# The last 128 maxima of a row-norm kernel: four small transposes and one 512-byte line for one transpose and four short rows

## Chip, cores, metric

One core of one Trainium2 chip. The metric is the time of one execution as measured on the device, in microseconds (us), from a few runs of each kernel. The trace's own span, from the program's first instruction to its last, is a little shorter. The runs list spans to 0.1 us, so a time minus span from a run without a trace is good to 0.05 us. The experiments ran on two chips (the fifth to the eighth on another than the rest), each beside the kernel before in the same rounds.

Some terms. A semaphore is a counter by which engines and copies tell one another that work is done; raising it is an increment. The issue of a copy is the instruction that starts it; the data move afterwards, in packets. The closing barrier is the meeting of all engines at the program's end. The TensorE clock was granted in full in every run.

## Reference

```python
def reference(x: np.ndarray) -> np.ndarray:      # x: 8192 x 8192 float32
    return np.linalg.norm(x, ord=np.inf, axis=1) # the largest |x| of every row
```

256 MiB (268.44 MB) are read, 32 KiB are written.

## The kernel before

Rows go to partitions, 128 at a time. 25 large loads (128 partitions x 16384 values) are followed by ever smaller ones, so that little is left to do when the last byte lands. Each load is reduced by one VectorE instruction. SyncE issues all DMA copies. The cuts of code below are shortened; `...` marks what is left out.

```python
class Pieces:
    ...
    def reduce(self, dst, src):
        i = len(self.reductions)
        ins = self.nc.vector.tensor_reduce(out=dst, in_=src, axis=X, op=max, apply_absolute_value=True)
        ins.wait_op(self.sems[i % SEMS], 16 * (i // SEMS + 1), "sem-ge")
        ...
```

The maxima of all rows but the last 128 are turned by TensorE and stored while the last pieces are still being reduced (`store_early`). The last 128 lie one per partition, in the first column of `last`, and are turned at the very end:

```python
    last_t = single.tile([P, 32], f32)
    make_identity(nc, ident)
    ...
    store_early()

    turn = nc.vector.transpose(out=last_t, in_=last)     # 4 blocks of 32x32
    pieces.after_loads(turn)
    tc.declare_fence(turn.ins, group="loads")
    nc.sync.dma_start(
        out=out_tail[n_tail - 1].rearrange("(b k) -> b k", k=32),
        in_=last_t.rearrange("(b c) k -> c b k", c=32)[0],   # partitions 0, 32, 64, 96
    )
```

A VectorE transpose turns every block of 32x32 by itself. So the 128 maxima end up as four rows of 32 values (128 B), in partitions 0, 32, 64 and 96, and go out as a 4x32 copy.

## Time and profile before

| | before |
|---|---|
| time, median of 4 runs | 630.83 us (630.74 to 630.91) |
| profiled run: time, span | 630.54 us, 628.346 us |
| VectorE busy | 88% |
| HBM read | 268.44 MB, 427 GB/s |
| instructions in VectorE's compiled program | 65 |

The lines that carry the reading stand in the prediction below: the loads fill the DMA engines to the end, VectorE keeps step, and after the last reduction a string of 2.76 us runs alone. From the view of the closing barrier's line in the kernel before (engine, operation, count: shortest/median/longest ns, start of the first and of the last in us; the q after the engine's name means its sequencer):

```profile
L224 DVEq EVENT_SEMAPHORE  x2: 21/21/21, 627.8 to 628.3; - x2
L224 PEldq EVENT_SEMAPHORE  x2: 51/51/51, 627.8 to 628.3; - x2
```

Every engine passes that barrier together.

### The profile page before, as it was taken

What the parts mean: (1) busy time and instruction counts of PE and PEld (TensorE: products, weight loads), DVE (VectorE), ACT (ScalarE), POOL (GpSimd) and SP (SyncE); (2) the same over time, 40 slices, a digit from 0 to 9 for tenths busy, and PEclk for the clock granted to TensorE, in tenths of its full rate; (3) what the DMA queues carried; (4) which work ended last, traced back from release to release, by engine and by line L of the source; (5) the groups of instructions that cost most, each with busy time, mean ns of one, the idle gap of its engine ahead of it and who ended that gap; (6) DMA issues with size and microseconds to landing.
All of it is one profiled execution on the core that took longest, in us unless ns stands there. A gap on an engine that the chain in (4) does not pass through costs nothing.

```text
span 628.3 us, 182 instructions
## 1 busy us (share of the span) xinstructions
PE 1.0 (0%) x3; PEld 0.3 (0%) x3; DVE 551.9 (88%) x54; ACT 2.0 (0%) x4; POOL 3.2 (1%) x15
## 2 busy tenths in 40 slices
PE   0000000000000000000000000000000000000000
PEld 0000000000000000000000000000000000000000
DVE  0588988889988889888898888998888999999998
ACT  0000000000000000000000000000000000000000
POOL 0000000000000000000000000000000000000000
DMA  9999999999999999999999999999999999999996
GB/s 401 401 467 401 467 401 467 401 467 401 467 401 467 401 467 401 467 401 467 401 467 401 467 401 467 401 467 401 467 401 434 434 434 434 434 414 428 424 424 281
DMA packets 7696, 268.47 MB, mean 427 GB/s; under 512 B 874, under 2 KB 912, under 8 KB 1936
## 3 DMA queue, kind: packets, MB, share of 16 engines
q1 hardware_dynamic: 7696, 268.47, 99.2%
HBM read 268.44 MB, written 0.03 MB: 427 GB/s over the span
## 4 chain that ended last, share of the span: by engine, by line
DMA 55%; DVE 44%; issue 0%; DVEq 0%
DMA ring<-in_x_dram 55%; DVE res_big L88 25%; DVE res_tail L88 10%; DVE parts L88 8%; DVE ring L88 1%; DVE last_t L194 0%; DVEq L88 0%
## 5 line engine op out<-in xcount | busy, mean ns | idle before, releaser
L88 DVE TENSOR_REDUCE res_big<-ring 128x2 f32<-128x16384 f32 x25 | 430.5, 17220 | 73.7 <-DMA ring<-in_x_dram 73.7
L88 DVE TENSOR_REDUCE res_tail<-ring 128x1 f32<-128x8192 f32 x7 | 60.2, 8675 | 0.0
L88 DVE TENSOR_REDUCE parts<-ring 128x1 f32<-128x4096 f32 (+5 forms) x15 | 52.2, 3555 | 0.0
L88 DVE TENSOR_REDUCE ring<-ring 128x1 f32<-128x1408 f32 (+4 forms) x6 | 9.1, 1566 | 0.1
L188 POOL TENSOR_SCALAR res_tail<-parts 128x1 f32<-128x1 f32 x6 | 1.7, 283 | 602.4 <-DVE parts L88 602.4
L151 ACT COPY line<-ps 25x128 f32<-25x128 f32 x2 | 0.5, 264 | 502.8 <-PE ps L150 502.8
L150 PE MATMUL ps<-ident,res_big 128*25 128x128 f32 x2 | 0.6, 402 | 504.4 <-DVE res_big L88 504.4
L151 ACT ACT_TABLE_LOAD x1 | 1.3, 1283 | 0.7 <-PEq L213 0.7
L188 POOL TENSOR_SCALAR parts<-parts 128x1 f32<-128x1 f32 x3 | 0.8, 282 | 10.7 <-DVE parts L88 10.7
L159 ACT COPY line_tail<-ps_tail 13x128 f32<-13x128 f32 x1 | 0.3, 255 | 112.1 <-PE ps_tail L157 112.1
L157 PE MATMUL ps_tail<-ident,res_tail 128*13 128x128 f32 x1 | 0.4, 391 | 112.0 <-POOL res_tail L188 112.0
L150 PEld LDWEIGHTS ps<-ident,res_big 128*25 128x25 f32 x2 | 0.2, 124 | 504.4 <-issue 504.4
masks.py:199 POOL TENSOR_SCALAR_AFFINE_SELECT ident<-ident 128x128 f32<-128x128 f32 x1 | 0.3, 294 | 0.1
L194 DVE STREAM_TRANSPOSE last_t<-ring 128x32 f32<-128x32 f32 x1 | 0.2, 211 | 0.0
masks.py:197 POOL MEMSET ident<- 128x128 f32 x1 | 0.2, 205 | 0.3 <-POOLq L213 0.3
L157 PEld LDWEIGHTS ps_tail<-ident,res_tail 128*13 128x13 f32 x1 | 0.1, 97 | 112.5 <-POOL res_tail L188 112.5
L213 POOL MEMSET const-uint8-127<- 128x1 uint8 x1 | 0.1, 103 | 0.0
L213 POOL MEMSET const-bfloat16-1.0<- 128x1 bf16 x1 | 0.1, 102 | 0.0
L213 POOL MEMSET const-float32-0.0<- 128x1 f32 x1 | 0.1, 99 | 0.2 <-issue 0.2
L213 POOL MEMSET const-float32-1.0<- 128x1 f32 x1 | 0.1, 99 | 0.0
## 6 DMA issues: line engine op xcount, KB each, us to landing
ring<-in_x_dram SPq DMA_DIRECT2D x7, 4096.0 KB, 40.5
ring<-in_x_dram SPq DMA_DIRECT2D x8, 2048.0 KB, 39.0
ring<-in_x_dram SPq DMA_DIRECT2D x2, 1216.0 KB, 27.7
ring<-in_x_dram SPq DMA_DIRECT2D x2, 864.0 KB, 23.3
ring<-in_x_dram SPq DMA_DIRECT2D x1, 1664.0 KB, 26.6
ring<-in_x_dram SPq DMA_DIRECT2D x2, 704.0 KB, 15.1
ring<-in_x_dram SPq DMA_DIRECT2D x1, 1248.0 KB, 20.9
ring<-in_x_dram SPq DMA_DIRECT2D x1, 1120.0 KB, 19.3
```

The source lines that it names most:

```text
L88: ins = self.nc.vector.tensor_reduce(out=dst, in_=src, axis=mybir.AxisListType.X, op=mybir.AluOpType.max, apply_absolute_value=True,)
L150: nc.tensor.transpose(ps, res_big[:, :, r], ident)
L151: nc.scalar.copy(out=line[:, :, r], in_=ps)
L157: nc.tensor.transpose(ps, res_tail, ident)
L159: nc.scalar.copy(out=line_tail, in_=ps)
L188: nc.gpsimd.tensor_scalar(out=dst, in0=best, scalar1=parts[i], scalar2=None, op0=mybir.AluOpType.max)
L194: turn = nc.vector.transpose(out=last_t, in_=last)
L213: nc = _bacc.Bacc("TRN2", target_bir_lowering=False, num_devices=1)
```

## The change

The intent: let the store be one full line of 512 B instead of four short ones. Four transposes of one 32x32 block each write side by side into 32 partitions, so that all 128 maxima come to lie in partition 0.

```diff
-    last_t = single.tile([P, 32], f32)
+    last_t = single.tile([32, P], f32)
...
-    turn = nc.vector.transpose(out=last_t, in_=last)
-    pieces.after_loads(turn)
+    for b in range(P // 32):
+        turn = nc.vector.transpose(
+            out=last_t[:, b * 32 : b * 32 + 32], in_=last[b * 32 : b * 32 + 32, :]
+        )
+        pieces.after_loads(turn)
     tc.declare_fence(turn.ins, group="loads")
     nc.sync.dma_start(
-        out=out_tail[n_tail - 1].rearrange("(b k) -> b k", k=32),
-        in_=last_t.rearrange("(b c) k -> c b k", c=32)[0],
+        out=out_tail[n_tail - 1].rearrange("(b k) -> b k", b=1),
+        in_=last_t[0:1, :],
     )
```

## The prediction

> **What bounds the kernel now.** I read the page's shares and its chain first, to see what kind of kernel this is; then the timeline and the chain of the last microseconds, because all that the diff touches runs there; then the DMA queue's own waits, for what follows the store.
>
> The page says that 268 MB are read and that the DMA engines are 90% busy or more in every slice but the last:
>
> ```profile
> DMA  9999999999999999999999999999999999999996
> HBM read 268.44 MB, written 0.03 MB: 427 GB/s over the span
> ```
>
> So the loads set the time almost to the end, and VectorE (88% busy) keeps step with them. A change behind the last load can touch only what lies behind it. That is the end of the timeline (start us, us, engine, line, operation, tiles):
>
> ```profile
> 617.70 0.33 SPq L160 DMA_DIRECT2D out_dram<-line_tail  x1
> 625.62 0.21 DVE L194 STREAM_TRANSPOSE last_t<-ring 128x32 f32<-128x32 f32 x1
> 625.86 0.60 SPq L197 DMA_DIRECT2D out_dram<-last_t  x1
> ```
>
> and of the chain that ended last:
>
> ```profile
> 616.49 7.71 DVE ring L88 x5
> 624.20 0.03 issue
> ...
> 624.30 1.30 DVE ring L88
> 625.60 0.02 issue
> 625.62 0.21 DVE last_t L194
> ```
>
> The reader should see two things. One: from 616 us on VectorE has no gap worth a name, so the last reduction ends at 625.6 because VectorE works, not because it waits (the semaphore of the last load is full at 624.04, before the last reduction starts at 624.30). Two: after it comes one serial string to the end of the span at 628.3: transpose, issue of the store, the store's journey, the closing barrier. Nothing lies beside it. The waits of the DMA queue show the journey and who waits for it:
>
> ```profile
> SPq L197 <- DVE last_t L194: 7.8, 1, 7.8
> SPq L160 <- ACT line_tail L159: 5.5, 1, 5.5
> SPq L224 <- DMA out_dram<-last_t: 0.9, 1, 0.9
> ```
>
> From the trace's single packets and semaphore events I take the string in finer steps (us from the span's start): transpose 625.622 to 625.833; issue 625.862 to 626.461; four packets of 128 B, which start at 627.090, 627.097, 627.118 and 627.150 and take 11 ns each, each followed by its 4-byte semaphore write, the last done at 627.167; their four increments seen at 627.417 to 627.481; the closing barrier goes on at 627.497 and ends at 628.346. Every part of the change is therefore paid or gained in full, and the whole string from 625.62 on is 2.7 us, 0.4% of the time. That is the frame: the time cannot move by 2% (12.6 us) unless something breaks.
>
> **What the Trainium skill says.** Four places.
> "VectorE: DVE Perf Modes", section "Two Vector instructions with no wait between them": an instruction is held until all earlier ones have finished if its input starts in another group of 32 partitions than the last input did (or its output than the last output). The four new transposes read partitions 0, 32, 64 and 96 on, so the second, third and fourth would be held. The trace of before has only the unheld kind: its last 1408-wide reduction but one runs 1.609 us and the next starts 1.527 us after its start, an overlap of 0.08 us.
> "DMA: Bandwidth & Descriptors", section "Why a DMA increments its semaphore by 16 and not by 1": the store's outer count sets how many engines carry it, and the issuing sequencer adds the rest. The trace agrees: 4 rows give four data packets, four increments by engines and one by the sequencer (626.87). One row should give one packet on one engine.
> The same page, "Specifications": writes under 512 B cost a read-modify-write. The trace has no equal write of 512 B with idle engines to compare with, so I can't tell what that costs here.
> "Perfetto Trace Analysis", section "DMA Instruction — HWDGE (DVE, Sync)": the profiled issue ends when the sequencer is done, and the data movement lies outside it. The trace agrees: the issue ends at 626.46, the first packet starts 0.63 us later.
>
> **The change, part by part.**
> The order of instructions against the kernel before shows nothing moved: the one 128x32 transpose becomes four 32x32 at the same place on VectorE, the store from 4x32 becomes 1x128, and all waits stay as they are; only the fourth transpose raises a semaphore, and the store waits for it.
>
> Transposes. A 32x32 transpose streams 32 elements per partition, as the 128x32 one did; with fewer partitions it should be no shorter, so 211 ns each. Held, one after another with the 20 to 35 ns that the trace shows between the last reduction and the transpose: three more at 211 + 25 = 0.24 us, sum +0.71 us. Not held, they would be one per (60 + 32 x 1.04 =) 93 ns, by the constants that the kernel's own author fitted for the reductions, which 1.527 us for 1408 columns confirms: sum +0.28 us. I lean to held, but the gap may be nearly nothing: +0.65 us.
>
> Issue of the store. The store of before is the dearest issue in the program: 599 ns. All others with an earlier wait take 327 to 376 ns, and the nearest in form, line_tail from 13 rows of consecutive partitions, takes 332. What sets last_t apart is that its four rows lie 32 partitions apart. The compiled programs differ there too: of the 56 DMA copies before, last_t's alone lacks a mark (ant_dge_precooked) that the others carry; after, it has it as well. So I expect about 330 ns: -0.27 us. This is the part that the change's words do not mention.
>
> The journey. One packet in place of four: the fourth one started 60 ns after the first, and that stagger goes; the one packet is 512 B, where 512-byte packets of loads took 27 to 29 ns against 11: net about -0.04 us. The confirmation (0.31 us from the end of a semaphore packet to its increment) I leave as it is. Whether a write of 512 B is confirmed sooner I can't size; I take 0 to -0.1 us, and put nothing in the sum.
>
> Sum: +0.65 - 0.27 - 0.04 = +0.34 us. On 630.75 that is 631.09; I shade it for the unsized confirmation and say 631.05.
>
> **The rivals.**
> The transposes overlap as the reductions do: +0.28 - 0.27 - 0.04 = -0.03 us, a tie at 630.7. For it: the reductions of before overlap by 0.08 us. Against: they never change partition group, these do.
> The store gains more than expected, because a full 512-byte line saves the read-modify-write that the change is after: with -0.3 us more the sum is +0.04 us, a tie again. For it: the string's longest pause, 0.9 us from issue to release. Against: of that 0.9 us, 0.63 us pass before the first packet starts, and the 0.31 us of confirmation are the most that could shrink.
> The issue does not become cheaper (599 ns may come from something else, such as the engines having gone idle since 624 us): +0.61 us, 631.35. For it: it is the only issue whose engines stood idle for over a microsecond. Against: the first loads of the program, also on idle engines, took 402 to 432.
> The loads themselves run otherwise in the new kernel: nothing in the order of instructions changes for them, so I give it no weight beyond the scatter of runs (630.74 to 630.91, and 630.54 in the profiled one).
>
> **Range and chances.** All rivals lie between -0.1 and +0.7 us; the scatter of one kernel adds some 0.2 on each side, and another chip or day may add a little more: 630.5 to 631.7. A move of over 2% would need 12.6 us, over four times the whole string behind the last reduction; I leave 1% on each side for what I have not seen.
>
> **What would show it.** Right: a group of four transposes at about 211 ns, the last one ending some 0.9 us after the last reduction (0.25 us before); an issue of about 330 ns for last_t; one packet of 512 B; a span of about 628.6 us. Wrong: transposes that start under 0.15 us apart (overlap, so no loss), an issue that still takes 0.6 us (then the row spacing is not what made it dear), or a confirmation clearly under 0.3 us (then the short writes did cost something). If the span differs by more than a microsecond, the loads have changed, and my frame is wrong.

## The result

| | before | after |
|---|---|---|
| time, median | 630.83 us (4 runs, 630.74 to 630.91) | 630.39 us (4 runs, 630.30 to 630.52) |
| profiled run: time | 630.54 us | 630.30 us |
| profiled run: span | 628.346 us | 628.620 us |
| time minus span | 2.194 us | 1.680 us |
| VectorE's program | 65 instructions | 68 instructions |

The ratio of the times is 0.9993 (95% interval 0.9976 to 1.0011): the same within 2%. Ratios here are the mean time of one kernel's fast runs over the mean of the other's in the same rounds, so not quite the ratio of the medians quoted. The predicted 631.05 was 0.66 us too high, and 630.39 lies 0.11 us below the predicted range.

The odd thing stands in the table: **the span became longer by 0.27 us, and the time shorter.** The profiled span came out where it was predicted (628.6), in part by luck: 0.10 of its +0.27 us is a later last reduction. What fell is the part of the time that lies outside the span.

From the timeline of the kernel after:

```profile
625.73 0.84 DVE L196 STREAM_TRANSPOSE last_t<-ring 32x32 f32<-32x32 f32 x4
626.59 0.23 SPq L201 DMA_DIRECT2D out_dram<-last_t  x1
```

The transposes take 0.84 us instead of 0.21, as foreseen, but the issue takes 0.23 us where 0.33 was expected and 0.60 was before. From the DMA queue's own waits in the kernel after:

```profile
SPq L201 <- DVE last_t L196: 8.4, 1, 8.4
SPq L228 <- DMA out_dram<-last_t: 0.8, 1, 0.8
```

The wait for the store to land is 0.8 us, 0.1 less than before. And from the closing barrier's line:

```profile
L228 DVEq EVENT_SEMAPHORE  x2: 21/21/21, 628.0 to 628.6; - x2
L228 PEldq EVENT_SEMAPHORE  x2: 51/51/51, 628.0 to 628.5; - x2
```

Here VectorE's last instruction starts at 628.6, the others' at 628.5; before, both were at 628.3. In the single events VectorE starts 0.13 us behind the other engines. That is a first hint at VectorE's instruction stream.

With the trace's single packets and semaphore events the string behind the last reduction can be added up, in us:

| piece | before | after | change |
|---|---|---|---|
| transposes, first start to last end | 0.211 | 0.840 | +0.629 |
| start of the store's issue to its first packet | 1.228 | 0.700 | -0.528 |
| first packet to end of the last | 0.077 | 0.036 | -0.041 |
| last packet to its increment | 0.314 | 0.328 | +0.014 |
| three short hand-overs | 0.079 | 0.078 | -0.001 |
| closing barrier, to the end of the span | 0.849 | 0.946 | +0.097 |
| time minus span | 2.194 | 1.680 | -0.514 |
| sum, from the end of the last reduction to the end of the time | 4.952 | 4.608 | -0.344 |

(In the profiled run of after the last reduction itself ended 0.104 us later, so the profiled times differ by only 0.24. The end of that reduction moves by 0.1 to 0.6 us from run to run of one kernel, with the loads. The sum of the last line is free of that, and I use it below as "the tail".) The time minus span lies behind the span: the last event on the semaphore by which the engines meet comes 2.314 us after the span's end before, and 1.807 us after it in the kernel after, a difference of 0.507 us.

So the change itself is nearly a tie inside the program (+0.17 us), and half a microsecond goes after its end. Why?

### The profile page after: what moved, and what is told of

Read it like the earlier page. It is cut to its first block, busy times and chain, and to the rows that moved or that the text cites. A ratio compares the mean times of both kernels' runs of the same rounds, so it can differ in the third digit from the quotient of the medians.

```text
span 628.6 us, 185 instructions
## 1 busy us (share of the span) xinstructions
PE 1.0 (0%) x3; PEld 0.3 (0%) x3; DVE 552.5 (88%) x57; ACT 2.0 (0%) x4; POOL 3.2 (1%) x15
## 4 chain that ended last, share of the span: by engine, by line
DMA 55%; DVE 44%; issue 0%; DVEq 0%
DMA ring<-in_x_dram 55%; DVE res_big L88 25%; DVE res_tail L88 10%; DVE parts L88 8%; DVE ring L88 1%; DVE last_t L196 0%; DVEq L228 0%; DVEq L88 0%
```

## The experiments

Theory A: VectorE's program is three instructions longer, and this moves the place at which its next block of instructions has to be fetched, from behind the closing barrier, where it delays everyone, to before it, where it is hidden. Theory B: it is the store, of which less is left to settle when the program ends. Every run lists time and span, so time minus span can be read in each.

### Three idle instructions, and nothing else

```diff
     make_identity(nc, ident)
+    pad = single.tile([P, 3], f32)
+    for i in range(3):
+        nc.vector.memset(pad[:, i : i + 1], 0.0)
```

> The kernel before with three memsets of one column on VectorE at the program's start, where VectorE waits for the first load: nothing of the last microseconds is touched, but VectorE's program is 68 instructions long as in the kernel after, not 65. The time measured on the device is longer than the span in the trace by 2.2 us before and by 1.7 us after. Theory (the gain is the place at which the longer VectorE program ends, nothing of the transposes or the store): span as before, 628.3 to 628.6, but time minus span falls to 1.7, so the time falls by about 0.5, to 630.3. Rival (the gain comes from the store, of which less is left to settle when the program ends): span and time as before, 630.8, time minus span 2.2.

Measured: 630.24 us (630.10 to 630.34) against 631.04 of the kernel before in the same rounds, ratio 0.9989 (0.9974 to 1.0004). Time minus span was 1.67 to 1.74 us in all four runs, against 2.14 to 2.26 in the seven runs of before. The timeline at the end is that of the kernel before, only shifted by 0.04 us:

```profile
625.66 0.21 DVE L197 STREAM_TRANSPOSE last_t<-ring 128x32 f32<-128x32 f32 x1
625.90 0.60 SPq L200 DMA_DIRECT2D out_dram<-last_t  x1
```

Old transpose, old store, short end. B falls, and of A the length of the program is borne out (that a fetch lies behind it is tested further below): three memsets that compute nothing, at the start of the program, make the whole gain outside the span. The interval of the ratio includes 1, so the times alone would not show it. The tail, free of the loads, is 4.541 us here against 4.952 before: the length is worth 0.41 us net, because 0.11 of the 0.52 outside comes back as a longer closing barrier.

### Half of the change at a time

The four transposes with the store of before:

```diff
-    turn = nc.vector.transpose(out=last_t, in_=last)
+    for b in range(P // 32):
+        turn = nc.vector.transpose(out=last_t[b * 32 : b * 32 + 32, :], in_=last[b * 32 : b * 32 + 32, :])
...
     nc.sync.dma_start(out=out_tail[n_tail - 1].rearrange("(b k) -> b k", k=32),
         in_=last_t.rearrange("(b c) k -> c b k", c=32)[0])
```

> The four transposes of the change alone, with the store of before (4 rows of 128 B, 32 partitions apart). Both theories: transposes 0.84 us instead of 0.21, issue of the store 0.6 us, so the span is 0.6 longer than before, about 629.0. Theory of VectorE's program length (68): time minus span 1.7, time about 630.7. Rival (the store): time minus span 2.2, time about 631.4.

Measured: 630.93 us against 631.04, time minus span 1.63 to 1.73.

```profile
626.14 0.85 DVE L196 STREAM_TRANSPOSE last_t<-ring 32x32 f32<-32x32 f32 x4
627.02 0.60 SPq L201 DMA_DIRECT2D out_dram<-last_t  x1
```

The span was 629.1 to 629.6, as expected or a little longer.

The store of the change with one transpose (three quarters of the line are zeros):

```diff
-    last_t = single.tile([P, 32], f32)
+    last_t = single.tile([P, P], f32)
     make_identity(nc, ident)
+    nc.gpsimd.memset(last_t[:, 32:P], 0.0)
...
-    turn = nc.vector.transpose(out=last_t, in_=last)
+    turn = nc.vector.transpose(out=last_t[:, 0:32], in_=last)
...
+    nc.sync.dma_start(out=out_tail[n_tail - 1].rearrange("(b k) -> b k", b=1), in_=last_t[0:1, :])
```

> The store of the change alone: one 128x32 transpose, then one line of 512 B, of which only the first 32 values are right (wrong on purpose; the rest is a memset to 0 early on GpSimd, which makes the programs of GpSimd and SyncE one instruction longer, VectorE's stays at 65). Issue 0.23 us, first packet 0.7 us after the issue starts instead of 1.23, so the span is about 0.55 shorter than before, 627.9. Theory of VectorE's program length: time minus span 2.2, time about 630.2. Rival (the store): time minus span 1.7, time about 629.7.

Measured: 630.22 us against 631.04, time minus span 2.14 to 2.23, span 627.9 to 628.5.

```profile
625.79 0.21 DVE L195 STREAM_TRANSPOSE last_t<-ring 128x32 f32<-128x32 f32 x1
626.09 0.23 SPq L198 DMA_DIRECT2D out_dram<-last_t  x1
```

With this the square is closed: old or new store, 65 or 68 instructions, and time minus span follows the number of instructions alone. In the tail, the transposes alone cost 0.64 us against the padded kernel before (5.183 to 4.541), and the new store alone gains 0.50 us against the kernel before (4.456 to 4.952), although its issue started 0.092 us after the transpose here and 0.029 before.

### What made the old store dear

The store of before, from partitions 0 to 3 instead of 0, 32, 64, 96:

```diff
-        in_=last_t.rearrange("(b c) k -> c b k", c=32)[0],
+        in_=last_t[0:4, :],
```

> The kernel before with its store of four 128 B rows taken from partitions 0 to 3 instead of 0, 32, 64, 96 (wrong on purpose). The compiled copy now carries the mark that all other copies carry. If the dear issue came from the missing mark or the row spacing: issue about 0.33 us instead of 0.60, first packet about 0.25 to 0.5 us earlier, span and time 0.3 to 0.5 lower. If it came from the number or the size of the rows: issue 0.6, nothing changes. Time minus span 2.2 by the theory of program length (VectorE 65).

Measured: 630.42 us against 631.04, time minus span 2.21 to 2.23.

```profile
626.25 0.25 SPq L197 DMA_DIRECT2D out_dram<-last_t  x1
```

Still four rows of 128 B, but the issue fell to 0.25 us and the first packet came 0.72 us after its start, not 1.23. Neither the number of rows nor their size was dear.

The same rows with the copy's mark switched off:

```diff
+    nc.dge_precook = False
     nc.sync.dma_start(
```

> The previous kernel (store from partitions 0 to 3, wrong on purpose) with the mark switched off for that one copy, so same rows, same sizes, adjacent, but unmarked. If the missing mark is what makes the issue dear: issue back at 0.60 us (marked: 0.25), first packet 1.22 us after the issue starts (marked: 0.72), span 0.5 above the marked one's. If the row spacing is: all as in the marked one. Time minus span 2.2 either way (VectorE 65 instructions).

Measured: 630.76 us against 630.75, first packet 1.32 us after the start of the issue, each 0.1 us more than expected (issue 0.70).

```profile
626.05 0.70 SPq L198 DMA_DIRECT2D out_dram<-last_t  x1
```

Same bytes, same rows, and all of the cost is back. (The mark is a flag that the build puts on a copy. Built once more, the two kernels' programs differ in one byte, in this copy's instruction.) So it is the missing mark in the compiled copy that is dear, and the spacing of 32 partitions because the build gave no mark to a copy with such rows; rows so spaced with the mark, in one copy, were not run. Its worth is 0.60 us up to the first packet for these rows, of which only 0.45 us (0.70 to 0.25) show in the issue's own duration.

### The length of VectorE's program

Two idle memsets, as above with 2 for 3:

> The kernel before with two idle memsets at VectorE's start, so 67 instructions. In the three kernels with 68, VectorE's very last instruction comes 0.13 us late, which none with 65 shows: if a block of instructions has to be fetched there, the fetch falls at the last instruction with 68, and with 67 or less behind the program's end, where it delays the closing work. Theory (a fetch at a fixed place of the stream): with 67 still time minus span 2.2, time as before, and no late last instruction. Rival (the delay falls gradually with length): time minus span about 1.85.

Measured: 630.66 us against 630.75, time minus span 1.94 to 2.00. Neither expectation was met to the number. The theory said 2.2 and the rival 1.85, so the passage from 2.2 to 1.7 is not one sharp step between 67 and 68: at 67 part of the delay is already gone. VectorE's last instruction was not late, as the theory said.

Twelve:

> The kernel before with twelve idle memsets at VectorE's start, so 77 instructions. Theory (a fetch at a fixed place): the fetch now falls among the last reductions, while earlier instructions run, so it is hidden wholly: time minus span 1.7 and no late last instruction, so the span is about 0.1 shorter than with three memsets, time 0.1 lower. Rival (only certain lengths are short, or the effect grows with length): time minus span 2.2 again, or well under 1.7. If the fetch delays a reduction, a gap of up to 0.5 us shows between the last reductions.

Measured: 631.52 us against 630.75, by the medians slower by 0.77 (ratio 1.0008, 0.9993 to 1.0023), though time minus span was 1.79 to 1.83 and VectorE's last instruction was not late. The part outside the span was 0.1 us above the theory's 1.7, but the 0.1 us by which the late last instruction lengthens the closing barrier with 68 is gone: barrier and outside together take 2.62 us here and 2.63 in the kernel after, against 3.04 before. The part inside the span did not meet the theory. A fetch of instructions now stands in the view of the DMA queues, where the kernel before has only q1 (queue, kind: packets, MB, share):

```profile
q1 hardware_dynamic: 7696, 268.47, 99.0%
q14 instruction: 1, 0.01, 0.0%
```

and among the waits after 560 us, where VectorE of the kernel before waits for no load:

```profile
DVE parts L88 <- DMA ring<-in_x_dram: 0.6, 2, 0.3
```

The fetch, one packet of 8192 B, starts at 564.2 us, amid the loads. The next load to land did so 3.09 us before its reduction started; in the kernel before it was 3.86. The loads behind it have little to spare (0.43 us, then 0.08 for the tightest), and so two reductions waited for their load. The two gaps, with the overlap lost, are 0.72 us. So what left the program's end was not free here: at the fetch the landing of the loads falls back by another 0.76 us against the kernel before (from 0.71 to 1.47), and stays there. That the fetch does this is argued from the moment, and how one packet of 0.33 us costs so much is not shown. The profiled span is longer by 1.48 us in all; the other 0.70 us arose by the fifth load, before 101 us. That is the scatter of the loads: the second run of the padded kernel below (3 memsets) fell back by 0.6 us between its third load and its sixth, with no fetch in its span.

Three memsets on GpSimd:

```diff
-        nc.vector.memset(pad[:, i : i + 1], 0.0)
+        nc.gpsimd.memset(pad[:, i : i + 1], 0.0)
```

> The three idle memsets on GpSimd instead of VectorE: GpSimd's program 39 instructions for 36, VectorE's 65. Theory (VectorE's length alone counts, because VectorE's fetch is the one that is not hidden): time minus span 2.2, time as before. Rival (any engine's longer program, or the memsets' work, does it): time minus span 1.7.

Measured: 630.73 us against 630.75, time minus span 2.15 to 2.22. It is VectorE's length that counts, not any memsets, and not GpSimd's. (In the version with two queues below, SyncE's and ScalarE's programs are longer too, and time minus span is that of 68.)

### Are the transposes held?

```diff
-            out=last_t[:, b * 32 : b * 32 + 32], in_=last[b * 32 : b * 32 + 32, :]
+            out=last_t[:, b * 32 : b * 32 + 32], in_=last[0:32, :]
```

> The kernel after with all four transposes reading partitions 0 to 31 (wrong on purpose: one quarter four times). In the kernel after they start 0.212 us apart. If they are held because each reads another group of 32 partitions than the one before: now not held, starts about 0.09 us apart, the four together 0.48 us instead of 0.84, span and time 0.36 lower. If a transpose never overlaps the one before: 0.212 apart, nothing changes. Time minus span 1.7 (VectorE 68).

Measured: 629.98 us against 630.74, ratio 0.9986 (0.9972 to 0.9999). The result was wrong on purpose, one quarter of the maxima four times, though close enough in value to pass the comparison with the reference.

```profile
625.77 0.48 DVE L196 STREAM_TRANSPOSE last_t<-ring 32x32 f32<-32x32 f32 x4
```

The starts are 0.135, 0.094 and 0.093 us apart instead of 0.212, 0.214 and 0.212. The change of the partition group is what keeps the four apart, and it costs 0.36 us of the change's 0.63. (The four also read the same bytes here; the two were not separated.)

### The two kernels at equal length, and a version meant to beat both

> The kernel after once more, on the same chip as the next two, to compare it with the kernel before at equal length of VectorE's program. Theory: time minus span 1.7, time 0.4 to 0.5 below before.

Measured: 630.24 us (630.21 to 630.58) against 630.74, ratio 0.9992 (0.9979 to 1.0005), time minus span 1.64 to 1.74.

> The kernel before with three idle memsets on VectorE, beside the kernel after on one chip: both have 68 instructions on VectorE. By the trace the change by itself costs 0.63 us in transposes, gains 0.53 up to the first packet and 0.04 in packets, so this one should be 0 to 0.15 us faster than the kernel after. If the change has a gain of its own beyond the program's length, the kernel after is faster than this one.

Measured: 630.40 us (630.36 to 630.95), time minus span 1.65 to 1.70. By the medians the kernel after is 0.16 us faster, against the expectation; behind the last reduction the traces have it slower. The last reduction ended at 626.2 us in the profiled run of this one and at 625.6 in the other, and the same program had run with its last reduction ending at 625.6 the first time; that is the scatter of the loads. Behind the last reduction the tail is 4.538 us here (4.541 the first time) and 4.616 in the kernel after (4.608 the first time): the change by itself costs 0.07 us. Single times can't resolve that; the traces agree with each other to 0.01.

```diff
     turn = nc.vector.transpose(out=last_t, in_=last)
...
+    row = out_tail[n_tail - 1].rearrange("(b k) -> b k", k=32)
+    for b in range(P // 32):
+        eng = nc.sync if b % 2 == 0 else nc.scalar
+        eng.dma_start(out=row[b : b + 1], in_=last_t[b * 32 : b * 32 + 1, :])
```

(and the three memsets on VectorE)

> A version meant to beat both: one 128x32 transpose as before, the four rows stored by four marked copies of 128 B, two issued by SyncE and two by ScalarE, and three idle memsets on VectorE. Each issue 0.23 us, so the last first-packet comes about 0.95 us after the transpose instead of 1.26: about 0.3 us below the padded kernel before, 629.95. Rival: the two queues' issues do not run beside each other, then 4 times 0.23 and no gain over the padded kernel before. Time minus span 1.7 in both, if the longer programs of SyncE and ScalarE do not matter.

Measured: 630.34 us (630.17 to 630.60), time minus span 1.70 to 1.77. The expected gain of 0.3 us did not come, as the rival said: the tail is 4.641 us, 0.10 more than the padded kernel's.

```profile
626.23 0.52 SPq L203 DMA_DIRECT2D out_dram<-last_t  x2
626.24 0.81 ACTq L203 DMA_DIRECT2D out_dram<-last_t  x2
```

ScalarE's first issue, begun 5 ns after SyncE's, took 0.558 us, over twice its second (0.218). The last of the four packets started 1.31 us after the transpose's end, as with the old store. The issues did run beside each other, unlike what the rival said, but the first of ScalarE's was stretched; what they share is not shown.

### Does the length act by blocks?

After these twelve runs it was still open why the length matters. If blocks are fetched, the effect has to come back with a period. The memsets at the start were raised to 128, 131, 256 and 259. The edit is that of the three idle memsets, with another count.

> The kernel before with 128 idle memsets at VectorE's start: 193 instructions. The trace's instruction fetches move 8192 B, which is 128 instructions of 64 B. If VectorE's stream is fetched in steps of 128 instructions, the step lies at the same place of the program's end as with 65: time minus span 2.2. If the steps are of 256 instructions, or the effect has nothing to do with fetched blocks, the step now lies at the start, among the memsets: time minus span 1.8, as with 77.

> 131 idle memsets, 196 instructions on VectorE: 128 more than the kernels with 68. Steps of 128: time minus span 1.7 and VectorE's last instruction 0.13 us late, as with 68. Steps of 256, or no blocks: 1.8, and no late last instruction.

> 256 idle memsets, 321 instructions on VectorE. Steps of 128 or of 256: time minus span 2.2 as with 65. No blocks at all: 1.8 as with 77.

> 259 idle memsets, 324 instructions on VectorE: 256 more than the kernels with 68. Steps of 128 or 256: time minus span 1.7 with a late last instruction; no blocks: 1.8 without one.

All kernels by the length of VectorE's program, over all their runs:

| VectorE instructions | kernels | time minus span, us | 8 KB fetches inside the span |
|---|---|---|---|
| 65 | before, one turn + line, adjacent rows (two), GpSimd memsets | 2.14 to 2.26 | 0 |
| 67 | 2 memsets | 1.94 to 2.00 | 0 |
| 68 | after (twice), 3 memsets (twice), four turns + old store, same group, two queues | 1.62 to 1.77 | 0 |
| 77 | 12 memsets | 1.79 to 1.83 | 1 |
| 193 = 65 + 128 | 128 memsets | 2.16 to 2.20 | 1 |
| 196 = 68 + 128 | 131 memsets | 1.71, 1.71 | 1 |
| 321 = 65 + 256 | 256 memsets | 2.16 to 2.18 | 2 |
| 324 = 68 + 256 | 259 memsets | 1.69 to 1.70 | 2 |

The fetches stand in the DMA queues' view of the kernels with 128, 131, 256 and 259 memsets (from 131 on it counts one packet of 24 B too):

```profile
q14 instruction: 1, 0.01, 0.0%
q14 instruction: 2, 0.01, 0.0%
q14 instruction: 3, 0.02, 0.0%
q14 instruction: 3, 0.02, 0.0%
```

and the late last instruction in the closing barrier's line, with 193 (first two lines) and 196:

```profile
L227 DVEq EVENT_SEMAPHORE  x2: 21/21/21, 628.5 to 629.0; - x2
L227 PEldq EVENT_SEMAPHORE  x2: 51/51/51, 628.5 to 629.0; - x2
L227 DVEq EVENT_SEMAPHORE  x2: 21/21/21, 628.3 to 628.9; - x2
L227 PEldq EVENT_SEMAPHORE  x2: 51/51/51, 628.3 to 628.8; - x2
```

The effect returns after 128 instructions, which at 64 B each (VectorE's compiled file has 4160 B for 65) is the 8192 B of a fetch, and every further 128 put one more fetch inside the span. VectorE's last instruction is late with 196 and 324 (by 0.09 and 0.07 us), as with 68 (by 0.11 to 0.14), and not with 193 and 321. A period of 128 is shown; that it is not shorter, such as 64, rests on the count of fetches. Steps of 256, and no steps at all, are out. The times were 631.28, 630.66, 632.32 and 632.00 us against 630.60 of before in the same round, which was one round each. The traces show where they lost: the first load, during which these fetches came (at 7 to 13 us), landed 0.67 and 0.41 us later than before with one fetch, and 1.53 and 1.51 with two; in the twelve runs above it moved by at most 0.14. The memsets run in the same stretch, so the two are not separated there.

The traces also record semaphore events behind the span's end, and these show the place of the delay. On the semaphore by which the engines meet there, one gap (between the fifth event and the sixth) is 0.51 us in the kernel before and 0.46 to 0.52 in all with 65, 193 and 321; it is 0.10 in all others. With 67 it is an earlier gap (third to fourth event) that is long, 0.24 us against 0.04. The other gaps agree to 0.01. So the delay is 0.41 us, at one step of that meeting; with 67 it stands at an earlier step, and with 68 VectorE is late already inside the span. The other 0.1 us by which time minus span falls with 68 is no gain: the late last instruction ends the span later, while the meeting starts where it did (1.12 us after the closing barrier goes on in the kernel before, 1.13 after).

The Trainium skill has a page that bears on this, "Runtime: NRT & Kernel Launch", section "Instruction fetch mechanics": each engine's sequencer fetches its stream in blocks while it executes, and crossing a border is "mostly hidden". These runs fit the mechanism, but not the size of the blocks that the page gives (last section). Here the crossing was not hidden when it fell behind the program's end: 0.41 us.

What stays open: which engine the long step belongs to, and what it waits for at the border; that it is VectorE waiting for instructions is argued from the length, the period and the fetches. The fetch that the traces record near the end begins after the delay (1.61 to 1.69 us after the span's end with 65, 193 and 321, 1.15 with 67, 0.62 to 0.87 with 68 and 196), not in it. And I have not shown why the step that is long with 67 is only half as long.

## Why the prediction was wrong

By its own steps:

- **The frame, "the whole string from 625.62 on".** Right about what lies inside the span, and about the size of the whole: nothing near 2%. Wrong in a thing it didn't say: it added changes of the span to the time, as if the remaining 2.2 us were a constant. They are not. This is the step that failed. The part outside the span fell by 0.51 us because VectorE's program grew from 65 to 68 instructions (0.41 us net of the later end of the span), and no term or rival of the prediction had this. The numbers were at hand: the time of the profiled run and its span differed by 2.2 us, and that three instructions are added stood in the diff.
- **Transposes, +0.65.** Measured +0.63: held, as the cited rule said, 0.200 us each with 0.012 us between. Without the change of partition group it would have been +0.27 (0.479 in place of 0.211), close to the +0.28 of the rival.
- **Issue, -0.27.** The cause was right (the mark, by the pair of adjacent rows), the size was off: -0.528 to the first packet. The issue itself fell to 0.227 us rather than 0.330, and the stretch from its end to the first packet, which I had taken as fixed at 0.63, fell to 0.47.
- **Journey, -0.04.** Measured -0.041 for the packets. The rival's hope for a quicker confirmation of a full 512 B failed: 0.328 us against 0.314. The intent of the change, a line of full size, gained nothing by its size.
- **Closing barrier.** Taken as unchanged; +0.097 by VectorE's late last instruction, the same border seen from inside. It only moves the span's end, and is taken back outside.

The sum inside the span was predicted as +0.34 and is +0.17 behind the last reduction (the better issue, less the later barrier). With -0.51 outside it the tail is -0.34. Of the 0.68 us between the predicted +0.34 and this -0.34, then, 0.42 are the closing barrier and the part outside taken together, and 0.26 are the issue's size. Had the length been the same in both, the change would have been a loss of 0.07 us.

## What to carry to other kernels

When a change is worth less than a microsecond, compare time and span separately, because the end of the program outside the span depended here on the length of VectorE's instruction stream (not on GpSimd's), and three instructions that do nothing moved it by half a microsecond here, 0.41 us of it net. Before crediting a data layout for such a gain, run the old kernel padded to the new one's instruction count. For a store that ends a chain, choose a shape that the build turns into a cheap issue, and look at the first packet, not at the issue's duration alone.

## What the Trainium skill lacked or had wrong

- "Runtime: NRT & Kernel Launch", section "Instruction fetch mechanics": it gives blocks of 16 KiB, 256 instructions. The fetches here are of 8192 B, and the effect on the time repeats with 128 instructions (65, 193, 321: 2.2 us outside the span; 68, 196, 324: 1.7). It says the cost is mostly hidden; here it was 0.41 us behind the program's end, and with a fetch amid the loads the next load landed 0.77 us later against its reduction.
- No page that I found says that a copy without the compiled mark (ant_dge_precooked) is dearer to issue: 0.70 us against 0.25 for the same four rows, first packet after 1.32 us against 0.72; nor that rows 32 partitions apart get no mark from the build (of 56 copies before, this one alone has none).
- "DMA: Bandwidth & Descriptors", section "Specifications": transfers under 512 B are said to be done as read-modify-write. No such cost shows in this store's confirmation: 0.314 us for four writes of 128 B, 0.328 us for one of 512 B.
